# GLA and SSD layers: short products put off by some weight chunks, gate columns two blocks at a time, last output projection with four column blocks at once

## The chip, the cores and the metric

The kernel runs on one core of a Trainium2 chip. The metric is the device time of one execution in microseconds (us). TensorE (PE) multiplies, VectorE (DVE) and ScalarE (ACT) work elementwise, SyncE (SP) issues the weight transfers.

## The reference

Four layers in a row, RWKV, GLA, SSD, RWKV, on 256 tokens of width 2048, all in fp32. Each layer normalizes x, shifts and scales it by a modulation computed from c (`ada_w`), runs its mixer and adds the result to x with a gate. The two mixers that the change touches, cut down:

```python
def gla_mixer(h, ...):             # 4 heads, keys 256, values 512, chunks of 64 tokens
    q, k, v, g, low = split(h @ w_in)
    scores  = (q e^(b - b_ref)) (k e^(b_ref - b))^T            # within a chunk, causal
    o       = scores v + (q e^b) state;  state = state * e^b_last + (k e^(b_last - b))^T v
    return (rms_normalize(o, head_g) * silu(g)) @ w_out

def ssd_mixer(h, ...):             # 64 heads of 64 in 8 groups, state 128, chunks of 128 tokens
    z, xbc, dt = split(h @ w_in)
    xs, bm, cm = split(silu(causal_conv4(xbc)))
    y = (cb * decay)(xs * dt) + (cm prev_state) e^acum + d_skip * xs       # cb = cm bm^T, causal
    y = rms_normalize(y * silu(z), per group of 512)
    return y @ w_out
```

## The kernel before

Every large product is fp32 in three parts: each operand is split into a high and a low half, and hi x hi, lo x hi and hi x lo are summed in one PSUM bank. A weight chunk is 4 k-tiles of 128 rows by 256 columns. SP fetches it (`load_w`, tile `raw`), ACT casts the high half (`split`, L338, tile `H`), DVE subtracts the low half (L340, tile `L`), and PE runs 24 matmuls of 128x256 (`prods`, L393). `H` and `L` have three buffers each, so the cast of a chunk waits until PE has read the chunk three before it. `jobs` takes a list of column blocks of 256 and walks over the k-tiles; `proj` cuts wide projections into blocks and calls `jobs` with one block at a time. A block is accumulated in a bank of `acc`, of which there are two; when its last chunk is issued, its `evac` empties the bank. After each chunk `tick` counts up and, by the table `PACE`, issues the next pieces of the modulation (a transfer from `ada_w` and an `adaacc` product on DVE, L304).

GLA runs head by head: projections of v, q and k, then the short products on five banks of their own (`b1`): scores, values and state (L1167 to L1198, outputs into `O`), a Newton root per token, the transposes of the scaled `O` (L1212), and after that the projection of g, whose `evg` multiplies silu(g) with the turned `O` and splits it into `ys` (L408, L409). SSD runs group by group: bc columns, conv, scores and decay products `M`, xs columns, conv, transposes (L1348), state and values (L1356 to L1370), then z's columns, whose `evz` empties a bank in two halves: ACT takes tanh into `cvt` (L1379), DVE multiplies with the bank (L1380) and with `yv` (L1381). The sum over squares (L1393), a Newton root on DVE (L1041 to L1049), its broadcast (`inv_rms`, L480, L483, L485), the scaling (L1397) and the split into `ys` follow. Heads or groups go in pairs: `paired` hands the eight `ys` tiles of two of them to `outproj`, eight column blocks of two chunks each, before the next part's g or z; the last pair's comes at the layer's end.

The text's order is a priority, not the order on the engines: a list scheduler places each instruction when its inputs and buffers are free by its own estimate, earlier text first. Each engine then runs its list strictly in that order.

Of the kernel before, what the change touches and what calls it, by code (L numbers as in the profile page):

```python
# [9 lines left out]
F32 = mybir.dt.float32  # L10
# [119 lines left out]
class Kern:  # L130
    def __init__(self, ctx, tc, A, out, layers=(0, 1, 2, 3), final=True):
# [15 lines left out]
        self.hold = False  # L147
        self.par = self.const.tile([P, NPAR], F32, name="par")
# [237 lines left out]

    def prods(self, ps, xt, hi, lo, xc, wc, first, last, tokens=False):

        for w, part in ((hi, 0), (hi, 1), (lo, 0)):
            lhs, rhs = w[:, wc], xt[:, part, xc]  # L390
            if tokens:
                lhs, rhs = rhs, lhs
            self.nc.tensor.matmul(ps, lhs, rhs, start=first and part == 0 and w is hi, stop=last and w is lo)  # L393

    def tick(self):

        self.tk += 1
# [18 lines left out]
    def outproj(self, wv, k0, ys, i, norm=None):  # L416
# [10 lines left out]
        for n0 in range(0, D, cols):  # L427
            def evac(j, ps, n0=n0):
# [10 lines left out]
            self.hold = bool(norm) and n0 == D - cols  # L439
            self.proj(wv, n0, cols, ys, evac, k0=k0)  # L440
# [669 lines left out]
    def paired(self, n, part, wout, i):  # L1110

        ys, k0, due = [], 0, []
        for g in range(n):
            ys += part(g, lambda: due and due.pop()())
            if g % 2:
                due.append(lambda ys=ys, k0=k0, norm=self.b1 if g == n - 1 else None:
                           self.outproj(wout, k0, ys, i, norm))
                ys, k0 = [], k0 + 8
        due.pop()()

    def gla_head(self, h, hs, win, bc, due, vt):
# [33 lines left out]
        self.proj(win, 1024 + 256 * h, 256, hs, evk)  # L1155


        HS = (slice(0, 64), slice(64, 128))
        ps = self.b1()
        for s in range(2):  # L1160
            for bi in range(2):
                i = slice((2 * s + bi) * C, (2 * s + bi + 1) * C)
                for kk in range(2):
                    for bj in range(2):
                        j = slice((2 * s + bj) * C, (2 * s + bj + 1) * C)
                        l, r = (ke, qe) if bi == bj else (kn, qs)
                        nc.tensor.matmul(ps[HS[bj], s * P + bi * C:s * P + (bi + 1) * C], l[:, kk, j], r[:, kk, i],  # L1167
                                         start=(kk == 0), stop=(kk == 1))
        sT = gu.tile([P, 2, P], F32, name="sT")
        nc.vector.tensor_scalar(out=sT.rearrange("p c t -> p (c t)"), in0=ps[:, 0:T], scalar1=3e38, scalar2=-3e38,  # L1170
                                op0=ALU.min, op1=ALU.max)
        nc.vector.tensor_tensor(out=sT, in0=sT, in1=self.c("tri128").unsqueeze(1).broadcast_to([P, 2, P]),
                                op=ALU.mult)

        d4 = dec.rearrange("p (k c) o -> p k c o", c=NCH)
        for t, c, o in ((kn, 0, 1), (qs, 3, 2)):
            t = t[:, :, c * C:(c + 1) * C]
            nc.vector.tensor_tensor(out=t, in0=t, in1=d4[:, :, o].broadcast_to([P, 2, C]), op=ALU.mult)

        kt = gu.tile([P, 2, P], F32, name="kt")  # L1180
        ps = self.b1()
        for kk in range(2):
            nc.tensor.transpose(ps[:, kk * P:(kk + 1) * P], kn[:, kk, 0:P], self.c("ident"))
        nc.scalar.copy(out=kt.rearrange("p a c -> p (a c)"), in_=ps[:, 0:T])

        O = gu.tile([P, 2, 512], F32, name="O", bufs=1)
        S = gu.tile([P, 2, 512], F32, name="S")
        for s in range(2):
            ps = self.b1()
            nc.tensor.matmul(ps, sT[:, s, :], vt[:, s, :], start=True, stop=s == 0)  # L1190
            if s:
                for kk in range(2):
                    nc.tensor.matmul(ps, qs[:, kk, P:], S[:, kk, :], start=False, stop=kk == 1)
            nc.scalar.copy(out=O[:, s, :], in_=ps)
            if not s:
                for kk in range(2):
                    ps = self.b1()
                    nc.tensor.matmul(ps, kt[:, kk, :], vt[:, 0, :], start=True, stop=True)  # L1198
                    nc.scalar.copy(out=S[:, kk, :], in_=ps)

        var = gu.tile([P, 2], F32, name="var")
        for tt in range(2):
            sq = gu.tile([P, 512], F32, name="osq", bufs=1)
            nc.scalar.activation(sq, O[:, tt, :], AF.Square)
            nc.vector.tensor_reduce(out=var[:, tt:tt + 1], in_=sq, op=ALU.add, axis=mybir.AxisListType.X)
        rs = self.rsqrt_tiny(var, 1.0 / 512, EPS, gu)
        oT = gu.tile([P, 4, T], F32, name="oT")
        for tt in range(2):
            nc.vector.tensor_scalar(out=O[:, tt, :], in0=O[:, tt, :], scalar1=rs[:, tt:tt + 1], scalar2=None, op0=ALU.mult)
            ps = self.b1()  # L1210
            for v in range(4):
                nc.tensor.transpose(ps[:, v * P:(v + 1) * P], O[:, tt, v * P:(v + 1) * P], self.c("ident"))  # L1212
            for v in range(4):
                nc.scalar.activation(oT[:, v, tt * P:(tt + 1) * P], ps[:, v * P:(v + 1) * P], AF.Copy,
                                     scale=self.p("gla_head_g", v))
# [10 lines left out]
        self.proj(win, 4096 + 512 * h, 512, hs, evg)  # L1226
# [61 lines left out]

    def ssd_group(self, g, hs, win, acd, tk, due):
        nc = self.nc  # L1290
# [4 lines left out]

        def conv_evac(t0, dst, step=1):
            def ev(j, ps):
                cp = su.tile([P, 2, T + 3], F32, name="cvp")
                nc.vector.memset(cp[:, :, 0:3], 0.0)
                nc.scalar.copy(out=cp[:, :, 3:], in_=ps)  # L1300
                for u in range(2):
                    self.conv(t0 + j + u * step, cp[:, u, :], dst[:, j + u, :])
            return ev
        self.proj(win, 8192 + T * g, T, hs, conv_evac(32 + g, bcx, 8))
# [4 lines left out]
                            .rearrange("p (h t) -> p h t", h=8))  # L1309

        ps = self.b1()
        for c in range(2):
            cs = slice(c * C, (c + 1) * C)
            nc.tensor.matmul(ps[:, cs], Bt[:, cs], Ct[:, cs], start=True, stop=True)
        cb = su.tile([P, 2, C], F32, name="cb")
        nc.vector.tensor_tensor(out=cb, in0=ps[:, 0:T].rearrange("p (c t) -> p c t", c=2),
                                in1=self.c("tri128").unsqueeze(1).broadcast_to([P, 2, C]), op=ALU.mult)
        ps = self.b1()
        nc.tensor.transpose(ps[:, 0:C], Bt[:, 0:C], self.c("ident"))
        bk = su.tile([P, C], F32, name="bk")  # L1320
        nc.scalar.copy(out=bk, in_=ps[:, 0:C])

        M = [None, None]
        for c in range(2):
            m = su.tile([P, 8, C], F32, name=f"M{c}", bufs=1)
            for h in range(8):
                nc.vector.tensor_scalar(out=m[:, h, :], in0=ab[:, h, c * C:(c + 1) * C],
                                        scalar1=tk[:, 2 + c, 8 * g + h:8 * g + h + 1], scalar2=0.0,
                                        op0=ALU.subtract, op1=ALU.min)
            nc.scalar.activation(m, m, AF.Exp)  # L1330
            nc.vector.tensor_tensor(out=m, in0=m, in1=cb[:, c, :].unsqueeze(1).broadcast_to([P, 8, C]), op=ALU.mult)
            M[c] = m

        ce = su.tile([P, 8, C], F32, name="ce", bufs=1)
        nc.scalar.activation(ce, ab[:, :, C:], AF.Exp)
        nc.vector.tensor_tensor(out=ce, in0=ce, in1=Ct[:, C:].unsqueeze(1).broadcast_to([P, 8, C]), op=ALU.mult)

        de = su.tile([P, 8], F32, name="de")
        nc.vector.tensor_tensor(out=de, in0=ab[:, :, C - 1], in1=tk[:, 2, HG], op=ALU.subtract)
# [132 lines left out]
```

## Time and profile before

| | |
|---|---|
| median of 3 runs | 2883.41 us (2878.49 to 2889.22) |
| profiled execution | 2887.0 us, span 2885.0 us, mean TensorE clock 0.952 |
| PE busy | 2686.2 us, 93% |
| DVE busy | 2212.4 us, 77% |
| ACT busy | 1392.8 us, 48% |
| GLA | about 905 to 1346 us of the span |
| SSD | about 1346 to 2080 us |

An engine's busy time is what its instructions took; a wait belongs to the instruction at the end of an idle stretch, with the instruction that released it. The clock is a share of full speed: a stretch at 0.50 runs its matmuls half as fast. PE 93% busy includes such stretches.

### The profile page before, as it was taken

How to read it: one execution, taken by the hardware profiler on the slowest of the kernel's cores; microseconds unless marked ns; L12 is line 12 of the kernel's file. 1: busy time of each engine (PE TensorE's matmuls, PEld its weight loads, DVE VectorE, ACT ScalarE, POOL GpSimd, SP SyncE). 2: the span in 40 equal slices, each digit the busy share in tenths (PEclk: the TensorE clock that was granted, in tenths of full speed). 3: DMA queues.
4: the chain of work that ended last, by engine and by line, in shares of the span. 5: the costliest groups of instructions: out<-in, count | busy, mean ns of one | idle time of the engine just before them, and what ended most of it. 6: DMA issues, size and time to landing. Idle time of an engine off the chain costs nothing.

```text
span 2885.0 us, 64064 instructions
## 1 busy us (share of the span) xinstructions
PE 2686.2 (93%) x26098; PEld 2505.1 (87%) x26098; DVE 2212.4 (77%) x3918; ACT 1392.8 (48%) x2315; POOL 154.6 (5%) x298
## 2 busy tenths in 40 slices
PE   6899999999987899988998999999889999999997
PEld 4789889887877899987988999999879988988887
DVE  5778777877788888877898788887668897666666
ACT  3475655433335454434544454554457756453333
POOL 0011110101000000000000000000000111010100
PEclk8899999999998999999999999999989999999999
DMA  9866557977677888976784767776557665585543
GB/s 348 308 231 190 176 161 261 347 266 278 207 261 244 293 285 291 324 268 197 277 294 161 242 219 228 224 226 216 167 171 236 230 208 190 178 297 194 207 132 108
DMA packets 239126, 673.68 MB, mean 234 GB/s; under 512 B 72272, under 2 KB 78416, under 8 KB 235760
## 3 DMA queue, kind: packets, MB, share of 16 engines
q1 hardware_dynamic: 217904, 580.84, 60.2%
q0 software_dynamic: 20928, 88.75, 8.5%
q8 instruction: 205, 3.36, 0.5%
q14 instruction: 89, 0.73, 0.1%
HBM read 620.66 MB, written 48.82 MB: 232 GB/s over the span
## 4 chain that ended last, share of the span: by engine, by line
PE 66%; DVE 8%; DMA 8%; issue 3%; ACT 2%; SPq 1%; POOL 0%; DVEq 0%; ACTq 0%; POOLq 0%
PE acc L393 53%; DMA raw<-in_ada_w 3%; DVE L L340 2%; PE g L785 2%; DVE adaacc L304 1%; ACT H L338 1%; PE b L897 1%; DMA raw<-in_gla_w_in 1%; DMA dx<-bd 1%; DMA raw<-in_rwkv_w_in 1%; PE b L866 1%; DMA raw<-in_rwkv_w_out 1%; PE b L873 1%; DMA sp<-yd 1%; PE b L1030 1%
## 5 line engine op out<-in xcount | busy, mean ns | idle before, releaser
L393 PE MATMUL acc<-xs,H 128*128 128x256 f32 x8480 | 1634.4, 291 | 36.5 <-ACT H L338 8.1
L393 PEld LDWEIGHTS acc<-xs,H 128*128 128x128 f32 x8480 | 1362.8, 196 | 69.3 <-ACT H L338 11.4
L393 PE MATMUL acc<-xs,L 128*128 128x256 f32 x4240 | 1230.6, 291 | 17.1 <-DVE L L340 16.2
L338 ACT CAST H<-raw 128x1024 fp32r<-128x1024 f32 (+1 forms) x706 | 718.0, 1018 | 854.9 <-PE acc L393 634.3
L340 DVE TENSOR_TENSOR L<-raw,H 128x1024 fp32r<-128x1024 f32 (+1 forms) x706 | 833.7, 1183 | 248.9 <-ACT H L338 234.0
L393 PEld LDWEIGHTS acc<-xs,L 128*128 128x128 f32 x4240 | 830.8, 196 | 31.1 <-DVE L L340 21.5
L304 DVE SCALAR_TENSOR_TENSOR adaacc<-raw,cact,adaacc 128x1024 f32<-128x1024 f32 x300 | 384.0, 1280 | 132.6 <-DMA raw<-in_ada_w 130.2
L393 PE MATMUL acc<-ys,H 128*128 128x256 f32 x1536 | 293.3, 291 | 12.2 <-DVE ys L409 4.9
L393 PEld LDWEIGHTS acc<-ys,H 128*128 128x128 f32 x1536 | 245.9, 195 | 22.0 <-issue 6.6
L393 PE MATMUL acc<-ys,L 128*128 128x256 f32 x768 | 222.1, 290 | 0.4 <-DVE L L340 0.4
L393 PEld LDWEIGHTS acc<-ys,L 128*128 128x128 f32 x768 | 149.6, 195 | 4.6 <-issue 3.6
L551 ACT ACTIVATE hn<-x,mod,omu 128x256 f32<-128x256 f32 x192 | 113.4, 599 | 1.5 <-DVE x L542 1.2
L431 DVE SCALAR_TENSOR_TENSOR x<-acc,mod,x 128x256 f32<-128x256 f32 x192 | 83.6, 477 | 35.7 <-PE acc L393 35.3
L393 PE MATMUL acc<-H,xs 128*128 128x256 f32 x512 | 97.1, 290 | 1.6 <-ACT vt L1078 1.6
L554 DVE SCALAR_TENSOR_TENSOR xm<-x,par,hn 128x256 f32<-128x256 f32 x192 | 88.6, 476 | 1.4 <-ACT hn L551 0.3
L393 PEld LDWEIGHTS acc<-H,xs 128*128 128x128 f32 x512 | 82.4, 197 | 3.1 <-ACT vt L1078 1.8
L393 PE MATMUL acc<-L,xs 128*128 128x256 f32 x256 | 73.8, 289 | 0.0
L785 PE MATMUL g<-abkp 64*128 64x128 f32 x768 | 65.8, 293 | 4.0 <-DVE G L823 2.7
L408 ACT CAST xs<-xm 128x256 fp32r<-128x256 f32 x128 | 50.9, 400 | 35.4 <-DVE xm L554 33.0
L785 PEld LDWEIGHTS g<-abkp 64*128 64x128 f32 x768 | 52.2, 190 | 15.8 <-issue 8.8
L1284 DVE SCALAR_TENSOR_TENSOR cva<-cvp,hcw,cva 128x256 f32<-128x256 f32 x144 | 64.9, 476 | 0.0
L278 DVE SCALAR_TENSOR_TENSOR adaacc<-raw,cact,adaacc 128x512 f32<-128x512 f32 x56 | 41.9, 748 | 27.5 <-DMA raw<-in_ada_w 23.0
(358 smaller groups left out, 3063.0 us busy)
## 6 DMA issues: line engine op xcount, KB each, us to landing
raw<-in_ada_w SPq DMA_DIRECT2D x384, 512.0 KB, 4.8
raw<-in_rwkv_w_in SPq DMA_DIRECT2D x256, 512.0 KB, 4.7
raw<-in_ssd_w_in SPq DMA_DIRECT2D x128, 512.0 KB, 4.4
raw<-in_gla_w_in SPq DMA_DIRECT2D x96, 512.0 KB, 5.2
raw<-in_ssd_w_out SPq DMA_DIRECT2D x64, 512.0 KB, 4.2
raw<-in_rwkv_w_out SPq DMA_DIRECT2D x48, 512.0 KB, 4.2
abkp<-kd POOLq DMA_DIRECT2D x16, 1024.0 KB, 7.3
raw<-in_gla_w_out SPq DMA_DIRECT2D x32, 512.0 KB, 4.9
```

Source lines behind the costliest of these rows:

```text
L278: nc.vector.scalar_tensor_tensor(out=acc, in0=raw[:, u, :], scalar=self.cact[:, k:k + 1], in1=acc, op0=ALU.mult, op1=ALU.add)
L304: nc.vector.scalar_tensor_tensor(out=acc, in0=raw, scalar=self.cact[:, k:k + 1], in1=acc, op0=ALU.mult, op1=ALU.add)
L338: nc.scalar.copy(out=hi, in_=raw[:, a:a + n])
L340: nc.vector.tensor_tensor(out=lo, in0=raw[:, a:a + n], in1=hi, op=ALU.subtract)
L393: self.nc.tensor.matmul(ps, lhs, rhs, start=first and part == 0 and w is hi, stop=last and w is lo)
L408: nc.scalar.copy(out=t[:, 0, :], in_=src)
L431: nc.vector.scalar_tensor_tensor(out=self.x[:, t, 1:], in0=ps[:, u, :], scalar=gate[:, t:t + 1], in1=self.x[:, t, 1:], op0=ALU.mult, op1=A ...
L551: nc.scalar.activation(t1, x[:, k, 1:], AF.Identity, scale=self.omu[:, col:col + 1], bias=self.mods[(i, 0)][:, k:k + 1])
L554: done[k] = nc.vector.scalar_tensor_tensor(out=xm, in0=x[:, k, 0:T], scalar=self.p("rwkv_mu", col), in1=t1, op0=ALU.mult, op1=ALU.add)
L785: self.nc.tensor.matmul(ps[h][:, n * C:(n + 1) * C], s[r, q, c * C:(c + 1) * C], t[r, q, c * C:(c + 1) * C], start=True, stop=True)
L866: nc.tensor.matmul(ps[r, n * H:(n + 1) * H], G[h][:, q, r], tk[:, 2, q, HS[h]], start=not c, stop=not c or h == 1)
L1284: nc.vector.scalar_tensor_tensor(out=a, in0=src[:, k:k + T], scalar=w[k], in1=a, op0=ALU.mult, op1=ALU.add)
```

## The change

- `tick` gets a list of parts that are put off: `put_off(n, part)` holds a part until n more chunks have been issued, `run_later()` runs all that are left.
- GLA: scores 1 tick after q and k, values and state 3, transposes of `O` 6.
- SSD: scores and `M` 3 ticks after bc; transposes of xs 3 ticks after xs, state 5, values 6; the sum over squares 3 ticks after z and the scaling 5, for which `inv_rms` is cut in two.
- g of GLA and z of SSD: one `jobs` call with both column blocks, chunk by chunk in turn, so that both `acc` banks fill together.
- Last `outproj` of GLA and of SSD: the first four column blocks in one call, two of them in two of the five `b1` banks (`pairs`), so that the last part's own `ys` are first needed after four chunks; what is put off is run when they are asked for.
- bc's transpose shares the bank of the SSD scores.

```diff
+    def put_off(self, n, part):
+        self.later.append((self.tk + n, part))
+    def run_later(self, tk=math.inf):
+        while self.later and self.later[0][0] <= tk:
+            self.later.pop(0)[1]()
...
-            self.proj(wv, n0, cols, ys, evac, k0=k0)
+        blocks = [(n0, cols, taker(n0), cols, False) for n0 in range(0, D, cols)]
+        if lead:
+            n = len(lead) + 2
+            self.jobs(wv, blocks[:n], ys, k0, banks=lead)
+            blocks = blocks[n:]
+        for block in blocks:
+            self.hold = bool(norm) and block is blocks[-1]
+            self.jobs(wv, [block], ys, k0)
...
+        def out(g, ys):
+            def rows(k):
+                if k >= len(ys[k // 4]) + k // 4 * 4:
+                    self.run_later()
+                return ys[k // 4][k % 4]
+            last = g == n - 1
+            self.outproj(wout, 4 * g - 4, Lazy(8, rows), i, self.b1 if last else None,
+                         self.pairs(self.b1, 2) if last else ())
...
+        self.put_off(1, scores)
+        self.put_off(3, lambda: box.append(values()))
+        self.put_off(6, lambda: turned(box[0]))
...
-        self.proj(win, 4096 + 512 * h, 512, hs, evg)
+        self.jobs(win, [(4096 + 512 * h + T * n, T, lambda _, ps, n=n: evg(2 * n, ps), T, False) for n in range(2)], hs)
...
+        self.put_off(3, scores)
...
+        self.put_off(3, turned)
+        self.put_off(5, states)
+        self.put_off(6, values)
...
-        self.proj(win, 512 * g, 512, hs, evz)
+        self.jobs(win, [(512 * g + T * n, T, lambda _, ps, n=n: evz(2 * n, ps), T, False) for n in range(2)], hs)
...
+        self.put_off(3, sums)
+        self.put_off(5, scaled)
```

How the lists of the engines change, at three places. First ACT at the end of z of SSD group 2, before (`H` is the cast of a weight chunk, `cvt` the read of half a z bank):

```order
948 L338 CAST H<-raw 128x1024 x13
949 L1379 ACTIVATE cvt<-acc 128x256
950 L338 CAST H<-raw 128x1024
951 L1379 ACTIVATE cvt<-acc 128x256
952 L1384 ACTIVATE ss<-yv 128x256
953 L338 CAST H<-raw 128x1024
954 L1387 ACTIVATE cva<-yv 128x256
955 L338 CAST H<-raw 128x1024 x2
```

and of the change:

```order
954 L339 CAST H<-raw 128x1024 x14
955 L1431 ACTIVATE cvt<-acc 128x256
956 L339 CAST H<-raw 128x1024
957 L1431 ACTIVATE cvt<-acc 128x256
958 L1436 ACTIVATE ss<-yv 128x256
959 L1431 ACTIVATE cvt<-acc 128x256
960 L1439 ACTIVATE cva<-yv 128x256
961 L1431 ACTIVATE cvt<-acc 128x256
```

The four reads of the group now stand together; between the first bank's two reads there is a cast as before, but z's two banks now close one chunk apart, before four.

DVE at the same place, before:

```order
1765 L340 TENSOR_TENSOR L<-raw,H 128x1024
1766 L1380 SCALAR_TENSOR_TENSOR cvt<-cvt,acc 128x256
1767 L1381 SCALAR_TENSOR_TENSOR yv<-cvt,yv 128x256
1768 L340 TENSOR_TENSOR L<-raw,H 128x1024
1769 L1380 SCALAR_TENSOR_TENSOR cvt<-cvt,acc 128x256
1770 L1381 SCALAR_TENSOR_TENSOR yv<-cvt,yv 128x256
```

and of the change:

```order
1768 L341 TENSOR_TENSOR L<-raw,H 128x1024 x4
1769 L1432 SCALAR_TENSOR_TENSOR cvt<-cvt,acc 128x256
1770 L305 SCALAR_TENSOR_TENSOR adaacc<-raw,cact,adaacc 128x1024
1771 L1433 SCALAR_TENSOR_TENSOR yv<-cvt,yv 128x256
1772 L341 TENSOR_TENSOR L<-raw,H 128x1024
1773 L1432 SCALAR_TENSOR_TENSOR cvt<-cvt,acc 128x256 x2
```

The first bank's second multiply (first of row 1773) stands behind one more L and, here, an adaacc.

PE at SSD's end, before (`ys` rows are output projection, `b` a `b1` bank, L1393 the sum over squares, L483 the broadcast of the root):

```order
9150 L393 MATMUL acc<-ys,L 128x256
9151 L393 MATMUL acc<-ys,H 128x256 x2
9152 L393 MATMUL acc<-ys,L 128x256
9153 L1393 MATMUL b_24519<-cst,ss 128x1 x2
9154 L483 MATMUL b_24540<-xm,cst 128x256
9155 L393 MATMUL acc<-ys,H 128x256 x3
```

and of the change:

```order
9166 L398 MATMUL acc<-ys,H 128x256 x2
9167 L398 MATMUL acc<-ys,L 128x256
9168 L1447 MATMUL b_24611<-cst,ss 128x1 x2
9169 L512 MATMUL b_24672<-xm,cst 128x256
9170 L398 MATMUL b_24511<-ys,H 128x256
9171 L398 MATMUL b_24512<-ys,H 128x256
```

The sum and the broadcast still stand next to each other, ahead of the group's own `ys`. Between z and the sum there are now four chunks of 24 matmuls, before two.

## Rows read from the trace of the kernel before

**Rows 1.** The page, busy times and shares of the span.

```profile
PE 2686.2 (93%) x26098; PEld 2505.1 (87%) x26098; DVE 2212.4 (77%) x3918; ACT 1392.8 (48%) x2315; POOL 154.6 (5%) x298
```

**Rows 2.** Stretches: from:to, length, busy (x count) by engine, clock, DMA, GB/s.

```profile
1284.00:1346.00 62.00, 57.13 (x404) 49.98 (x404) 40.71 (x54) 24.51 (x43) 0.00 (x0) 0.89 0.65 210
1430.00:1600.00 170.00, 154.04 (x1269) 147.48 (x1268) 144.90 (x278) 81.33 (x122) 1.59 (x3) 0.94 0.68 232
1600.00:1700.00 100.00, 100.00 (x836) 98.10 (x837) 77.59 (x121) 47.86 (x67) 0.00 (x0) 1.00 0.70 228
2040.00:2080.00 40.00, 31.21 (x236) 28.70 (x235) 25.56 (x52) 15.06 (x25) 0.00 (x0) 0.83 0.45 150
```

**Rows 3.** Waits of PE, 1276 to 1300: total us, times, longest.

```profile
PE b L1212 <- DVE O L1209: 3.3, 1, 3.3
PE acc L393 <- ACT ys L408: 2.6, 2, 2.3
PE acc L393 <- DVE ys L409: 1.6, 1, 1.6
PE acc L393 <- DVE gth L1222: 0.5, 1, 0.5
```

**Rows 4.** Stretches of the clock, columns as in rows 2.

```profile
1285.10:1298.70 13.60, 8.84 (x36) 7.86 (x36) 8.66 (x14) 4.20 (x14) 0.00 (x0) 0.50 0.57 187
2063.30:2066.70 3.40, 3.40 (x18) 3.40 (x17) 1.97 (x3) 0.42 (x1) 0.00 (x0) 0.50 0.67 224
2070.10:2080.40 10.30, 6.31 (x24) 5.33 (x25) 4.84 (x19) 1.97 (x5) 0.00 (x0) 0.50 0.17 52
295.20:298.60 3.40, 3.40 (x19) 3.40 (x18) 3.30 (x13) 3.34 (x10) 0.15 (x1) 0.50 0.10 11
1006.00:1012.00 6.00, 6.00 (x54) 6.00 (x53) 5.34 (x9) 3.49 (x11) 0.00 (x0) 1.00 0.87 313
```

**Rows 5.** Timeline at SSD's end: start, length, engine, line, instruction, idle before and releaser.

```profile
2060.30 1.04 ACT L338 CAST H<-raw 128x1024 fp32r<-128x1024 f32 x1 [1.55 <-issue]
2061.25 0.38 ACT L1379 ACTIVATE cvt<-acc 128x256 f32<-128x256 f32 x1
2061.38 1.23 DVE L340 TENSOR_TENSOR L<-raw,H 128x1024 fp32r<-128x1024 f32 x1 [0.85 <-ACT H L338]
2062.52 0.41 DVE L1380 SCALAR_TENSOR_TENSOR cvt<-cvt,acc 128x256 f32<-128x256 f32 x1
...
2062.99 0.55 PE L393 MATMUL acc<-ys,H 128*128 128x256 f32 x2 [2.65 <-DVE cvt L1380]
...
2072.38 1.19 PE L483 MATMUL b<-xm,cst 128*128 128x256 f32 x2 [4.43 <-DVE xm L480]
...
2074.99 0.80 PE L393 MATMUL acc<-ys,H 128*128 128x256 f32 x2 [1.42 <-ACT ys L408]
```

**Rows 6.** Waits of PE, 1600 to 2040.

```profile
PE acc L393 <- DVE L L340: 0.4, 1, 0.4
```

**Rows 7.** The page, costliest groups: busy us, mean ns, idle before.

```profile
L304 DVE SCALAR_TENSOR_TENSOR adaacc<-raw,cact,adaacc 128x1024 f32<-128x1024 f32 x300 | 384.0, 1280 | 132.6 <-DMA raw<-in_ada_w 130.2
```

**Rows 8.** Timeline of PE at 293 and at 1005.

```profile
293.38 0.69 PE L1011 MATMUL b<-Tn,LT 32*32 32x32 f32 x16 [2.03 <-DVE Tn L995]
...
1005.38 0.50 PE L393 MATMUL acc<-H,xs 128*128 128x256 f32 x2 [1.62 <-ACT vt L1078]
```

**Rows 9.** Timeline of PE and DVE, SSD groups 0 and 1.

```profile
1437.84 0.50 PE L393 MATMUL acc<-xs,H 128*128 128x256 f32 x2 [1.26 <-DVE cvt L1380]
...
1512.19 0.50 PE L393 MATMUL acc<-xs,H 128*128 128x256 f32 x2 [2.84 <-DVE cvt L1380]
1513.25 2.35 DVE L1331 TENSOR_TENSOR M<-M,cb 128x1024 f32<-128x1024 f32 x2
1515.52 1.42 DVE L409 TENSOR_TENSOR ys<-yv,ys 128x256 fp32r<-128x256 f32 x4
...
1531.17 0.51 PE L393 MATMUL acc<-xs,H 128*128 128x256 f32 x2 [1.55 <-ACT cvp L1300]
```

More of the change, by code (lines that the diff above doesn't have):

```diff
@@ L385, in jobs, with pairs @@
                     evac(0, bank[:, 0:nj])
+    def pairs(self, bank, n):
+        return [bank().rearrange("p (j t) -> p j t", j=2) for _ in range(n)]
     def prods(self, ps, xt, hi, lo, xc, wc, first, last, tokens=False):
@@ L414, in parts, with outproj @@
         return t
-    def outproj(self, wv, k0, ys, i, norm=None):
+    def outproj(self, wv, k0, ys, i, norm=None, lead=()):
         nc = self.nc
@@ L425, in outproj, with taker, evac @@
         cols = 2 * P
-        for n0 in range(0, D, cols):
-            def evac(j, ps, n0=n0):
+        def taker(n0):
+            def evac(j, ps):
                 for u in range(ps.shape[1]):
@@ L1155, in gla_head @@
         self.proj(win, 1024 + 256 * h, 256, hs, evk)
[L1158 to L1168, printed above, removed]
@@ L1180, in gla_head @@
[L1180 to L1184, printed above, removed]
+        sT = gu.tile([P, 2, P], F32, name="sT")
         O = gu.tile([P, 2, 512], F32, name="O", bufs=1)
-        S = gu.tile([P, 2, 512], F32, name="S")
-        for s in range(2):
+        oT = gu.tile([P, 4, T], F32, name="oT")
@@ L1189, in gla_head, with scores @@
+        def scores():
+            HS = (slice(0, 64), slice(64, 128))
             ps = self.b1()
[L1190 to L1209, printed above, removed]
-            ps = self.b1()
[L1211 to L1215, printed above, removed]
+            for s in range(2):
+                for bi in range(2):
+                    i = slice((2 * s + bi) * C, (2 * s + bi + 1) * C)
+                    for kk in range(2):
+                        for bj in range(2):
+                            j = slice((2 * s + bj) * C, (2 * s + bj + 1) * C)
+                            l, r = (ke, qe) if bi == bj else (kn, qs)
+                            nc.tensor.matmul(ps[HS[bj], s * P + bi * C:s * P + (bi + 1) * C], l[:, kk, j], r[:, kk, i],
+                                             start=(kk == 0), stop=(kk == 1))
@@ L1287, in conv, with conv_evac, ev @@
         nc.vector.scalar_tensor_tensor(out=dst, in0=th, scalar=1.0, in1=a, op0=ALU.add, op1=ALU.mult)
+    def conv_evac(self, t0, dst, step=1):
+        nc = self.nc
+        def ev(j, ps):
+            cp = self.su.tile([P, 2, T + 3], F32, name="cvp")
+            nc.vector.memset(cp[:, :, 0:3], 0.0)
+            nc.scalar.copy(out=cp[:, :, 3:], in_=ps)
+            for u in range(2):
+                self.conv(t0 + j + u * step, cp[:, u, :], dst[:, j + u, :])
+        return ev
     def ssd_group(self, g, hs, win, acd, tk, due):
@@ L1294, in ssd_group @@
         bcx = su.tile([P, 2, T], F32, name="bc")
[L1296 to L1304, printed above, removed]
+        self.proj(win, 8192 + T * g, T, hs, self.conv_evac(32 + g, bcx, 8))
         Bt, Ct = bcx[:, 0, :], bcx[:, 1, :]
@@ L1319, in ssd_group @@
-        nc.tensor.transpose(ps[:, 0:C], Bt[:, 0:C], self.c("ident"))
         bk = su.tile([P, C], F32, name="bk")
[L1321 to L1332, printed above, removed]
+        M = [su.tile([P, 8, C], F32, name=f"M{c}", bufs=1) for c in range(2)]
@@ L1346, in ssd_group, with states, values @@
+        yv = su.tile([P, 4, T], F32, name="yv")
+        def states():
             ps = self.b1()
+            nc.tensor.matmul(ps, bk, xd.rearrange("p h d -> p (h d)"), start=True, stop=True)
+            nc.scalar.copy(out=xd.rearrange("p h d -> p (h d)"), in_=ps)
+        def values():
             for v in range(4):
-                nc.tensor.transpose(ps[:, v * P:(v + 1) * P], xT[:, v, c * C:(c + 1) * C], self.c("ident"))
-            t = su.tile([P, 8, 64], F32, name=f"xc{c}")
-            nc.vector.tensor_tensor(out=t, in0=ps.rearrange("p (h d) -> p h d", d=64),
-                                    in1=tk[:, c, HG].unsqueeze(2).broadcast_to([P, 8, 64]), op=ALU.mult)
@@ new lines, in values @@
+                hr = [(2 * v + u, slice(64 * u, 64 * u + 64)) for u in range(2)]
+                for h, r in hr:
+                    nc.tensor.matmul(ps[r, 0:C], xc[0][:, h, :], M[0][:, h, :], start=True, stop=True)
+                for h, r in hr:
+                    nc.tensor.matmul(ps[r, C:T], xc[1][:, h, :], M[1][:, h, :], start=True, stop=False)
+                for h, r in hr:
+                    nc.tensor.matmul(ps[r, C:T], xd[:, h, :], ce[:, h, :], start=False, stop=True)
+                nc.vector.scalar_tensor_tensor(out=yv[:, v, :], in0=xT[:, v, :], scalar=self.p("ssd_d", 4 * g + v),
+                                               in1=ps[:, 0:T], op0=ALU.mult, op1=ALU.add)
```

155 lines of the change are left out of this document (99 added, 56 removed).

## The prediction

> **What bounds the kernel now.** I read the busy times of the page first: PE works 93% of the span, DVE 77%, ACT 48% [rows 1]. So only PE's idle time and its clock can be saved, and the table by stretches says where they are. From 1600 to 1700 us, in SSD, PE is busy for all of the stretch at clock 1.00 (836 matmuls in 100 us: 0.120 us each, 2.9 us for a weight chunk of 24); nothing is to be won there, and any new wait is a loss in full. Time is lost at 1284-1346 (end of GLA), 1430-1600 (SSD groups 0 and 1) and 2040-2080 (end of SSD) [rows 2].
>
> The waits give the sizes. At GLA's end PE waits 3.3 + 2.6 + 1.6 + 0.5 = 8.0 us [rows 3], and the clock then stands at 0.50 for 13.6 us [rows 4], of which half, 6.8, is lost. At SSD's end it waits 2.65, 4.43 and 1.42 [rows 5], 8.5 in all, with 3.4 + 10.3 us at 0.50 [rows 4]: 6.9 lost. In the busy middle of SSD, from 1600 to 2040 us, one wait of 0.4 us is all [rows 6].
>
> The row that decides my forecast is the wait of 2.65 us that ends at 2062.99 [rows 5]. There z's second block of columns is followed by only one chunk into the other bank, 24 matmuls, before the next block wants the bank back. The bank is emptied in two halves, and by the order on the two engines the second half comes after a weight cast: ACT casts H at 2060.30 and reads the bank at 2061.25, DVE subtracts L at 2061.38 and only then, at 2062.52, does the second multiply; PE starts at 2062.99. A cover of 24 matmuls does not suffice where the usual 96, 11.5 us, do.
>
> **The change part by part.** PE's matmuls, the weight chunks and the pace of the modulation stay, so its 384 us of adaacc on DVE [rows 7] stay too. What changes is order.
>
> *g of GLA and z of SSD, two blocks chunk by chunk.* Both banks now close within one chunk of each other, and the next job wants the first one 24 matmuls after it closed. This is the situation at 2062.99, now at the ends of GLA heads 0, 1, 2 and of SSD groups 2 to 6, eight times, and in the changed order ACT's second read stands behind one more cast, which waits for the buffer of the last chunk, and DVE's second multiply behind that L. Price of one: from the cast's start at 2060.30 to PE's at 2062.99 it is 2.69 us [rows 5]; the buffer comes free two matmuls, 0.24, before the chunk's end, which leaves 2.45. The wait measured 2.65, and I take that: 8 x 2.65 = 21.2 (bounds 19.6 and, with an adaacc of 1.28 [rows 7] in the way at two places, 23.8). The waiting matmul holds all of PE behind it; the casts after it need buffers that PE gives back, so nothing runs ahead meanwhile.
>
> *The clock after these waits.* After the wait of 2.65 us the granted clock fell to 0.50, the lower level of 1.2 GHz, for 3.4 us; the same followed a wait of 2.03 us at 293; after 1.62 us at 1005 it stayed at 1.00 [rows 4, 5, 8]. So one new wait costs 0 or 1.7 us more. By the nearer rows most fall; I take six of eight: 10.2 (bounds 0 and 13.6). The Trainium skill, "TensorE: Matmul & The Clock Gate", section "A second HAM failure mode: psum-queue depth-cycling", says that a kernel which cycles through banks and leaves PE idle briefly between groups swings between the two levels and pays at each swing; the rows at 293 and 2062.99 agree, the one at 1005 does not, and by the rule this term would be 13.6.
>
> *SSD group 0.* z's bank already costs 1.26 us at 1437.84 [rows 9]; in the new order a cast, an L (1.23) and an adaacc (1.28) stand ahead of the second multiply: 1.04 + 1.23 + 1.28 + 0.41 is about 4 us from the last chunk's end [rows 5, 7], +2.7, and a clock fall of 1.7. Bounds 0 and +4.4.
>
> *SSD group 1.* Before, PE waits 2.84 us for the second multiply, until 1512.19, and the M products come after it [rows 9]. The new order puts both M products (2.35), four ys differences (1.42), two xc products and two Ls (2 x 1.23) ahead of it, 6.2 us without xc; PE would resume about 8 us after it is ready, +5, and the wait of 1.55 that ends at 1531.17 goes: +3.4. Bounds 0 and +6. The waits at about 1410, 1457 and 1566 keep their places and causes in the order: 0, plus or minus 2.
>
> *GLA's end.* Turning O is put off by six ticks and the four-block lead gives 96 matmuls of cover instead of 24. But the order keeps the transposes behind only 24 ys matmuls, and the new bank wait stands ahead of these: 2.65 us in place of 3.3. The rest of the chain is then covered by 48 more matmuls; I leave 0.5 + 0.7 for H and L cast late and 1.8 for the second g bank, late behind an adaacc. Idle 8.0 becomes 5.6: -2.4. The long stretch at half clock should split into short ones, 5 us in all: -4.3. Together -6.7 (bounds 0, if the waits only change places, and -14.8, 8.0 + 6.8, if all goes).
>
> *SSD's end.* 96 matmuls now stand between z and the group's own ys, the first 48 in banks of their own, so the wait of 2.65 and its 3.4 us at half clock go: -4.3. But the sum over the squares stands behind all 96 in PE's queue, with the broadcast of the inverse root as the next instruction: the chain sums, Newton steps, broadcast, yv, ys still runs while PE has nothing else. The 4.43 and 1.42 stay, with their 10.3 us at 0.50. Bounds 0 and -15.4 (8.5 + 6.9: all gone).
>
> *Put-off scores, values, states elsewhere.* They land in stretches that are 100% busy on PE: 0. The last RWKV layer's order shifts a little: 0, plus or minus 5.
>
> **Sum.** +21.2 + 10.2 + 4.4 + 3.4 - 6.7 - 4.3 = +28.2 us. The profiled execution took 2887.0 us (span 2885.0), 3.6 above the median: 2887.0 + 28.2 - 3.6 = 2911.6. Forecast 2911.
>
> **Rivals.** *A, faster.* The lead covers both ends and the bank waits stay away, because z's first half is emptied while the second block's last chunk runs. For it: in the middle of SSD DVE was rarely late [rows 6]. Against it: the 2.65 us that the same order of the queues cost [rows 5], and the cast can't be earlier, since its buffer is in use. The page "Perfetto Trace Analysis" of the Trainium skill, "Matmul Optimizations", speaks for A: it wants all banks in use, and the lead takes four where two were; its section "Matmuls" speaks against it, since groups are to rotate through banks so that emptying one overlaps the next group, and two banks that close together don't. The time: both ends by their far bounds, -30, with groups 0 and 1 at 0: 2853; with the ends at my values, -11: 2872. Chance 0.13.
> *B, no change that counts.* The bank waits come at 2.45 us, the clock stays up after all but one (+1.7), groups 0 and 1 cost 3 together, and the ends give 18: 19.6 + 1.7 + 3 - 18 = +6: 2890. For it: the wait of 1.62 us without a fall [rows 8]. Decided by whether the Newton chain at SSD's end gets cover. Chance 0.22.
> *C, worse.* Every wait pulls the clock, groups 0 and 1 at their upper bounds, the ends only change places: 23.8 + 13.6 + 10.4 - 4.3 = +43.5: 2927. Chance 0.15.
> *My forecast*, bank waits of about 2.6 us with most of them followed by half clock: 0.50.
>
> **How the numbers follow.** What a measurement of this kernel can tell from no change is about 0.5%, 14.4 us: the bounds are 2869 and 2898. Of A about two in ten lies between 2869 and 2872: faster 0.11. B is within, and of the forecast's own spread (2896 to 2922) a small part: same 0.25. The rest of the forecast and C: slower 0.64. The range leaves out A and the far end of C: 2880 to 2928.
>
> **What would show it.** In the profile after: PE's waits in SSD groups 2 to 6 on "DVE cvt", five of 2.3 to 2.8 us, where there was one of 0.4 on anything; three on "DVE gth" in GLA; short dips of the granted clock behind most. At SSD's end no wait on cvt, but one of 4 to 5 us on xm. At GLA's end a wait on gth of 2 to 3 us in front of the first ys, and little or none at the transposes of O. PE's busy time at full clock unchanged. I am wrong if PE stays 100% busy from 1600 us to SSD's end, or if the wait on xm is gone.

## The result, and the profile after

The changed kernel takes 2929.4 us (median of 4 runs, 2926.8 to 2934.7) against 2886.3 for the kernel before beside it; the ratio is 1.0156, 95% interval 1.0129 to 1.0182. It is slower by about 43 us. The forecast was 2911 with a range to 2928: the direction and the place were right, the size fell short, and the time lies just outside the range.

The profiled execution of the changed kernel took 2934.7 us (span 2932.8), 47.7 longer than the one before. Cut at the broadcasts of the layers' norms, and at the end of the span, the lengths in us are:

| | RWKV, first | GLA | SSD | RWKV, last | rest |
|---|---|---|---|---|---|
| before | 887.1 | 469.0 | 775.9 | 740.7 | 12.2 |
| after | 886.7 | 477.9 | 803.4 | 751.7 | 13.0 |
| difference | -0.4 | +8.9 | +27.5 | +11.0 | +0.8 |

The page's busy times say little of it: PE's is 13 us longer in a span that is 48 us longer, and the other engines work as they did [rows 1]. The clock alone does not explain it: the time at 0.50 is 84 us before and 100 after in GLA and SSD, and 279 against 275 in the whole program.

```profile
PE 2698.9 (92%) x26098; PEld 2507.7 (86%) x26098; DVE 2215.9 (76%) x3918; ACT 1390.8 (47%) x2315; POOL 154.0 (5%) x298
```

The waits do. PE's waits in the changed kernel from 900 to 1320 us (GLA's heads and end; `gth` is what g's bank is read into, as `cvt` for z's); columns: us in total, times, longest:

```profile
PE acc L398 <- DVE gth L1267: 8.3, 4, 2.6
```

and from 1320 to 2140 us (SSD):

```profile
PE acc L398 <- DVE cvt L1432: 29.7, 7, 7.5
PE b L512 <- DVE xm L505: 10.5, 2, 6.3
PE b L1398 <- DVE xT L1332: 4.7, 2, 3.3
PE b L398 <- ACT ys L422: 2.8, 1, 2.8
```

From 1600 to 2100 us, the busy middle of SSD, where one wait of 0.4 us stood [rows 6], there are now:

```profile
PE acc L398 <- DVE cvt L1432: 17.2, 5, 4.6
PE acc L398 <- DVE L L341: 1.0, 1, 1.0
```

And the stretch that was 100% busy [rows 2] has 64 matmuls fewer in it (stretch, length, busy and count of PE, PEld, DVE, ACT, POOL, clock, DMA, GB/s):

```profile
1600.00:1700.00 100.00, 95.79 (x772) 94.25 (x772) 71.14 (x123) 45.34 (x62) 0.53 (x1) 0.97 0.65 211
```

The timeline at the end of z of SSD group 3 shows what one such wait is (start, length, engine, line, instruction, idle before and releaser):

```profile
1722.20 1.04 ACT L339 CAST H<-raw 128x1024 fp32r<-128x1024 f32 x1
...
1723.14 0.37 ACT L1431 ACTIVATE cvt<-acc 128x256 f32<-128x256 f32 x1
...
1724.36 1.04 ACT L339 CAST H<-raw 128x1024 fp32r<-128x1024 f32 x1
1724.41 0.41 DVE L1432 SCALAR_TENSOR_TENSOR cvt<-cvt,acc 128x256 f32<-128x256 f32 x1
1724.86 0.43 DVE L1433 SCALAR_TENSOR_TENSOR yv<-cvt,yv 128x256 f32<-128x256 f32 x1
1725.31 0.38 ACT L1431 ACTIVATE cvt<-acc 128x256 f32<-128x256 f32 x1
1725.43 1.23 DVE L341 TENSOR_TENSOR L<-raw,H 128x1024 fp32r<-128x1024 f32 x1
...
1726.58 0.75 DVE L1432 SCALAR_TENSOR_TENSOR cvt<-cvt,acc 128x256 f32<-128x256 f32 x2
1727.04 0.50 PE L398 MATMUL acc<-xs,H 128*128 128x256 f32 x2 [2.65 <-DVE cvt L1432]
```

It is the wait of [rows 5] again, to the hundredth of a microsecond: the bank's first half is read at 1723.14, the second at 1725.31 behind a cast, and multiplied at 1726.58 behind that cast's L. At the end of group 6 the same order holds one thing more:

```profile
2023.86 1.28 DVE L305 SCALAR_TENSOR_TENSOR adaacc<-raw,cact,adaacc 128x1024 f32<-128x1024 f32 x1 [1.83 <-DMA raw<-in_ada_w]
2025.07 0.41 DVE L1433 SCALAR_TENSOR_TENSOR yv<-cvt,yv 128x256 f32<-128x256 f32 x1
2025.40 1.22 DVE L341 TENSOR_TENSOR L<-raw,H 128x1024 fp32r<-128x1024 f32 x1
...
2026.54 0.74 DVE L1432 SCALAR_TENSOR_TENSOR cvt<-cvt,acc 128x256 f32<-128x256 f32 x2
2027.00 0.80 PE L398 MATMUL acc<-xs,H 128*128 128x256 f32 x2 [4.64 <-DVE cvt L1432]
```

A step of the modulation stands on DVE in front of all that is left of the emptying, and it waits 1.83 us for its own weights to arrive. DVE takes its instructions in order, so the bank, and PE, wait for a transfer that has nothing to do with them.

### The profile page after: what moved, and what is told of

It is laid out like the page before. It is cut to its first block, busy times and chain, and to the rows that moved or that the text cites. A ratio compares the mean times of both kernels' runs of the same rounds, so it can differ in the third digit from the quotient of the medians.

```text
span 2932.8 us, 64075 instructions
## 1 busy us (share of the span) xinstructions
PE 2698.9 (92%) x26098; PEld 2507.7 (86%) x26098; DVE 2215.9 (76%) x3918; ACT 1390.8 (47%) x2315; POOL 154.0 (5%) x298
## 4 chain that ended last, share of the span: by engine, by line
PE 59%; DVE 11%; DMA 11%; issue 4%; ACT 2%; SPq 1%; POOL 0%; DVEq 0%; ACTq 0%; POOLq 0%
PE acc L398 46%; DMA raw<-in_ada_w 6%; DVE L L341 4%; DVE adaacc L305 2%; PE g L814 2%; ACT H L339 1%; DMA dx<-bd 1%; PE b L398 1%; DMA raw<-in_rwkv_w_out 1%; PE b L926 1%; DMA raw<-in_gla_w_in 1%; PE b L895 1%; PE b L902 1%; SPq L1001 0%; DVE xs L423 0%
## 5 line engine op out<-in xcount | busy, mean ns | idle before, releaser
L398 PE MATMUL acc<-ys,H 128*128 128x256 f32 x1408 | 268.6, 290 | 6.8 <-DVE gth L1267 5.2
L398 PEld LDWEIGHTS acc<-ys,H 128*128 128x128 f32 x1408 | 224.3, 194 | 17.0 <-issue 9.0
L398 PE MATMUL acc<-ys,L 128*128 128x256 f32 x704 | 203.2, 289 | 0.0
L398 PEld LDWEIGHTS acc<-ys,L 128*128 128x128 f32 x704 | 136.1, 193 | 3.5 <-issue 3.3
L814 PEld LDWEIGHTS g<-abkp 64*128 64x128 f32 x768 | 52.2, 190 | 17.2 <-issue 9.4
```

Source lines behind the costliest of these rows:

```text
L814: self.nc.tensor.matmul(ps[h][:, n * C:(n + 1) * C], s[r, q, c * C:(c + 1) * C], t[r, q, c * C:(c + 1) * C], start=True, stop=True)
```

## The experiments

Each time is a median; the ratio is to the kernel before, run beside it on the same chip, with its 95% interval. Layer lengths are from the profiles, one execution each.

**One block after the other.** Everything else of the change stays, with shorter put-offs, which this order needs.

```diff
-        self.put_off(6, lambda: turned(box[0]))
+        self.put_off(4, lambda: turned(box[0]))
-        self.jobs(win, [(4096 + 512 * h + T * n, T, lambda _, ps, n=n: evg(2 * n, ps), T, False) for n in range(2)], hs)
+        self.proj(win, 4096 + 512 * h, 512, hs, evg)
-        self.put_off(5, states)
-        self.put_off(6, values)
+        self.put_off(4, states)
+        self.put_off(4, values)
-        self.jobs(win, [(512 * g + T * n, T, lambda _, ps, n=n: evz(2 * n, ps), T, False) for n in range(2)], hs)
+        self.proj(win, 512 * g, 512, hs, evz)
```

> The change, but g of GLA and z of SSD one column block after the other as before; so that their inputs are there in time, the transposes of O are put off by 4 ticks instead of 6, SSD states and values by 4 instead of 5 and 6. Theory of the prediction (the two banks that close together cost the time): no wait on cvt or gth of over 1 us in SSD groups 2 to 6 and GLA heads 0 to 2; the time falls by 25 to 40 us, to 2890 to 2905, or lower if the ends gain. Rival (put-off products crowd DVE, or the lead costs): stays at 2920 or more. If the last RWKV layer's 11 us more in the profile come from its changed order and not from chance, they may stay here: 2895 to 2905.

Measured: 2887.4, ratio 1.0019 [1.0001, 1.0036]; GLA 466.9, SSD 777.8 us. No wait for `cvt` stands between 1600 and 2060 us. Without the pairs the loss is gone, but for 0.2%.

**The pairs alone, in the kernel before.**

```diff
-        self.proj(win, 512 * g, 512, hs, evz)
+        self.jobs(win, [(512 * g + T * n, T, lambda _, ps, n=n: evz(2 * n, ps), T, False) for n in range(2)], hs)
```

and the same for g.

> The kernel before with nothing of the change but g and z two column blocks chunk by chunk. Theory: waits on cvt of 2.6 to 4.8 us at SSD groups 2 to 6 as in the changed kernel, and the time rises by 25 to 45 us, to 2910 to 2930. Rival (put-offs and lead cost the time): within 8 us of before, 2880 to 2894.

Measured: 2918.9, ratio 1.0123 [1.0099, 1.0148]; GLA 479.6, SSD 804.0 us, as in the changed kernel. The waits for `cvt` are 27.7 us in eight. The pairs alone make most of the loss.

**The pair in two other banks.** The two blocks go to two of the five `b1` banks, so the next job does not want their banks.

```diff
-        ..., T, False) for n in range(2)], hs)
+        ..., T, False) for n in range(2)], hs, banks=self.pairs(self.b1, 2))
```

> The change, but the pair of g or z blocks is summed in two of the five b1 banks and not in the acc banks, so that the next job finds its bank free; order of the chunks and put-offs stay. Theory: the waits on cvt and gth at the next job's first matmul go, and with them the half clock behind them; time 2885 to 2900 unless short products now wait for the three banks that are left (waits on b). Rival (the chunk order itself or the put-offs cost): 2920 or more.

Measured: 2880.6, ratio 0.9997 [0.9982, 1.0012]; GLA 462.9, SSD 774.0 us. That is below the 2885 to 2900 expected. No wait for `cvt` or `gth` is left. In sum the order chunk by chunk costs nothing; what costs is that the next block wants the bank back 24 matmuls later. One new wait stood in SSD, on the modulation's sum:

```profile
1479.69 1.08 PE L311 MATMUL mx<-adaacc,cst 128*32 128x256 f32 x8 [9.48 <-DVE adaacc L305]
```

**Without the lead of four blocks.**

```diff
-                         self.pairs(self.b1, 2) if last else ())
+                         ())
```

> The change without the four-block lead in the last output projection of GLA and SSD (one column block at a time). Prediction's terms: at SSD's end the wait on cvt of about 2.7 us comes back with 3.4 us of half clock, at GLA's end the chain of ys; 5 to 11 us slower than the changed kernel, 2934 to 2941. Rival, the lead gives nothing (its chain still stands behind it in PE's list): within 4 us of 2929.

Measured: 2922.1, ratio 1.0136 [1.0107, 1.0166], beside 1.0156 [1.0129, 1.0182] for the whole change. Both expectations missed: without the lead the kernel is not slower but, if anything, faster, though the intervals overlap. The wait for `cvt` at SSD's end is back, 2.61 us at 2096.76; SSD takes 806.5 against 803.4 us, GLA 477.6 against 477.9. What the lead brings is at most some 3 us at SSD's end and nothing at GLA's. The last RWKV layer takes 738.6 us in this profile against 751.7, more than the lead's share; more on that layer at the end of the account below.

**z's bank emptied in one round.** One tanh and one multiply over both halves; GLA is left as it was.

```diff
+            both = su.tile([P, 2, T + 3], F32, name="cvp")[:, :, 0:T]
+            nc.scalar.activation(both, ps, AF.Tanh, scale=0.5)
+            nc.vector.scalar_tensor_tensor(out=both, in0=both, scalar=1.0, in1=ps, op0=ALU.add, op1=ALU.mult)
             for u in range(2):
                 v = j + u
-                th = su.tile([P, T], F32, name="cvt")
-                nc.scalar.activation(th, ps[:, u, :], AF.Tanh, scale=0.5)
-                nc.vector.scalar_tensor_tensor(out=th, in0=th, scalar=1.0, in1=ps[:, u, :], op0=ALU.add, op1=ALU.mult)
+                th = both[:, u, :]
```

> The changed kernel, with z's bank in the SSD groups emptied by one tanh and one multiply over both halves (512 columns each) in place of two of each over 256; GLA as it was. Theory (the bank is late because its emptying is two rounds on ACT and DVE, and a weight's cast or subtraction, or a modulation step, comes between the rounds): at most one of these is left ahead of each of the two instructions, so by the rows 1.04 + 0.6 + 1.23 + 0.75 = 3.6 us after the last product against 2.9 us of products in the other bank. The six waits for cvt (29.7 us in the changed kernel's profile) fall to under 1 us each, most falls of the clock behind them go, the SSD layer comes from 803 to about 780 us and the time from 2929 to 2900-2912. Rival (two banks that close 2.9 us apart are too few however they are emptied): the waits stay at 2 us and more, and the time at 2922-2932.

Measured: 2893.3, ratio 1.0032 [1.0015, 1.0049]; SSD 772.7 us, shorter than before the change, GLA 479.0 as in the changed kernel. The theory holds, and the time lies below the range that it gave; of the bank waits two are left, one of 1.7 us where under 1 was expected. The waits of PE from 1600 to 2060 us:

```profile
PE acc L398 <- DVE L L341: 2.3, 3, 1.2
PE acc L398 <- DVE cvp L1430: 2.1, 2, 1.7
```

and the end of z of group 2:

```profile
1639.42 1.05 ACT L339 CAST H<-raw 128x1024 fp32r<-128x1024 f32 x1 [1.83 <-PE acc L398]
...
1640.37 0.59 ACT L1429 ACTIVATE cvp<-acc 128x512 f32<-128x512 f32 x1
...
1640.50 1.23 DVE L341 TENSOR_TENSOR L<-raw,H 128x1024 fp32r<-128x1024 f32 x1 [1.66 <-ACT H L339]
...
1641.64 0.68 DVE L1430 SCALAR_TENSOR_TENSOR cvp<-cvp,acc 128x512 f32<-128x512 f32 x1
...
1642.47 0.47 PE L398 MATMUL acc<-xs,H 128*128 128x256 f32 x2
```

One cast, one tanh, one L, one multiply: from 1639.42 to 1642.32 that is 2.90 us, the length of the 24 matmuls that cover it, and PE goes on. The same cover that was 2.65 us short with two rounds suffices here with one. The Trainium skill, "Perfetto Trace Analysis", section "Optimizing Scalar/DVE Operations", says that grouping into larger operations can pay where the engine is saturated; here neither engine is (DVE 76% busy, ACT 47% in the changed kernel), and the two instructions were shortened by little (0.59 for twice 0.38, 0.68 for twice 0.41). What went is the cast and the L that the order puts between two rounds, 2.3 us.

**The modulation halted during z's pair.**

```diff
+        self.hold = True
         self.jobs(win, [(512 * g + T * n, T, lambda _, ps, n=n: evz(2 * n, ps), T, False) for n in range(2)], hs)
+        self.hold = False
```

> The changed kernel, with the modulation's steps halted during the eight chunks of each SSD group's z pair, and made up behind them at no more than two a chunk. Theory (waits above 2.65 us are a modulation step on DVE that itself waits for its transfer, or a step that stands in the row ahead of the emptying): groups 2 and 6 fall from 4.2 and 4.6 to 2.3-2.9, groups 0 and 1 (5.1 and 7.5) fall too, and the others stay at 2.6-3.1; the sum of the waits comes from 29.7 to about 16-20, the time from 2929 to 2914-2922. Rival (the steps made up later are late elsewhere, at the group's BC convolution or the transposes): the sum of all PE waits in the layer stays, and so does the time, 2925-2932.

Measured: 2917.6, ratio 1.0118 [1.0085, 1.0152]. The time lies where the theory put it, but the interval overlaps that of the changed kernel, and in the profile, which is of the longest of the four executions, SSD takes 804.8 us, no less than there. The sum of the waits for `cvt` fell as expected, to 18.9 us, and groups 0 and 1 have none; but the two waits of groups 2 and 6 grew: the first step after the halt is issued right at the end of z, where its weights are still on their way.

```profile
1648.53 1.28 DVE L305 SCALAR_TENSOR_TENSOR adaacc<-raw,cact,adaacc 128x1024 f32<-128x1024 f32 x1 [2.74 <-DMA raw<-in_ada_w]
...
1651.67 0.58 PE L398 MATMUL acc<-xs,H 128*128 128x256 f32 x1 [5.56 <-DVE cvt L1432]
...
2025.44 1.28 DVE L305 SCALAR_TENSOR_TENSOR adaacc<-raw,cact,adaacc 128x1024 f32<-128x1024 f32 x1 [3.56 <-DMA raw<-in_ada_w]
...
2028.58 0.80 PE L398 MATMUL acc<-xs,H 128*128 128x256 f32 x2 [6.66 <-DVE cvt L1432]
```

So the run is not shown to be a cure, but it is a dose of the suspected cause. In the changed kernel, group 2:

```profile
1652.77 1.28 DVE L305 SCALAR_TENSOR_TENSOR adaacc<-raw,cact,adaacc 128x1024 f32<-128x1024 f32 x1 [1.38 <-DMA raw<-in_ada_w]
...
1655.91 0.80 PE L398 MATMUL acc<-xs,H 128*128 128x256 f32 x2 [4.20 <-DVE cvt L1432]
```

Four pairs are at hand, the step's wait for its transfer and PE's wait for the bank: 1.38 and 4.20, 1.83 and 4.64 in the changed kernel, 2.74 and 5.56, 3.56 and 6.66 here. PE's wait is 2.8 to 3.1 us longer than the transfer's in each. The runs with the pairs alone, without the lead and with short put-offs give six more, with transfer waits of 1.11 to 1.95 us, and PE's is 2.8 us longer in all of them. A fifth place of this run, group 4, has the step ahead of the bank's first multiply, not the second: 1.38 and 3.74, 2.4 longer. In the changed kernel a wait without a step in between is 2.6 to 3.1 us, so the step's wait counts in full and of its 1.28 us of work little shows. The rival, that the waits come back elsewhere, is right for SSD in this profile.

**Shorter put-offs, the rest as changed** (4 in place of 6 in GLA, 4 and 4 in place of 5 and 6 in SSD).

> The changed kernel with shorter put-offs, turned after 4 chunks in place of 6 in GLA, states and values after 4 in place of 5 and 6 in SSD: the control to the single-block run, which needed these. Theory (put-offs are worth nothing either way, the pairs are all): 2925-2932, waits for cvt and gth as in the changed kernel, about 38 us together. Rival (the long put-offs, which bring the group's results close to z's evacuation, are part of the loss): under 2918.

Measured: 2929.9, ratio 1.0158 [1.0122, 1.0194]; waits for `cvt` 28.8 us in seven, for `gth` 8.0 in four. No effect of the put-offs' length is seen, so the single-block run is to be read as the pairs alone.

**Other banks, and the halt.** The pair in two `b1` banks, with the halt above.

> The kernel with the pair in two banks of b1, plus the modulation halted during each SSD group's z pair. In the run without the halt one new wait stood in the SSD layer: PE reached the modulation's sum (mx) 9.5 us before DVE had finished it, with 13.7 us at half clock. Theory (that wait is the modulation falling due among group 0's work on DVE, and goes when it is moved): 2864-2872, faster than both kernels. Rival (DVE is behind there whatever the order, and PE meets the wait at the next instruction that needs DVE): 2876-2884.

Measured: 2881.2, ratio 0.9996 [0.9977, 1.0014]. The rival holds. The wait on the modulation's sum went and came back as a wait of 8.5 us on `xm`, the operand of the broadcast of a group's root, here group 0's; SSD takes 785.7 us in this profile, longer than without the halt. The one-round run has such a wait at group 1's root, 8.64 us at 1567.82. This fits that DVE is behind by that much in groups 0 and 1, 85% busy from 1430 to 1600 us [rows 2], and that PE pays for it at whichever instruction needs DVE next.

**Both cures.** GLA's pair in two `b1` banks, z's bank in SSD in one round.

> The changed kernel with both of the cures that worked alone: GLA's pair in two banks of b1 (GLA took 462.9 us with it), and z's bank in SSD emptied over both halves at once (SSD took 772.7 us with it). Theory (each layer keeps its own result): 2883 - 6 - 3 = about 2874, 2868-2880, faster than both kernels by a little. Rival (the layers' differences of 3 to 6 us are within what single profiles of the same instructions differ by): 2880-2886, the same as the kernel before.

Measured: 2874.5, ratio 0.9977 [0.9959, 0.9995]; GLA 462.5, SSD 772.5 us. It is faster than both kernels, than before by 0.2%, which is less than half of what was called a measurable difference ahead of the result; 12 runs of it and 23 of before make the interval, which just leaves out 1.

**One round alone, in the kernel before.**

> The kernel before with one edit alone: z's bank in the SSD groups emptied over both halves at once. Theory (before, a bank has 96 products, over 10 us, until it is wanted again, so how it is emptied costs nothing): 2878-2886, the same, SSD at 774-778 us. Rival (the shorter emptying is a gain by itself on the two groups whose cvt waits stood there, 6.8 us in three, and at the SSD end): 2868-2876.

Measured: 2880.5, ratio 0.9995 [0.9975, 1.0015]. The same time, as the theory said. In its profile SSD is shorter (764.6 us), for which the rival spoke, and the last RWKV layer longer (750.4); the medians show no gain, though the interval has room for 0.25%. Behind the pairs the same edit brought the ratio from 1.0156 to 1.0032. So one round is worth that much only where the next block wants the bank 24 matmuls later.

## Why the prediction was right in direction and short in size

What a stretch costs is counted here by how late a kernel starts its n-th matmul, in profile time, against the n-th of the kernel before; all have 26098. The places are times of the kernel before.

*The bank waits (+21.2): the mechanism was right, the sum partly by luck.* In SSD they stand where they were put, and the experiments show the cause from three sides: other banks remove them, one round all but removes them, the pairs alone make them. SSD groups 2 to 6 wait 17.2 us where 13.25 was the sum for five, because in groups 2 and 6 the adaacc in the way waits for its transfer. The order had shown that adaacc between the two multiplies, and the bound took only its 1.28 us of work: the wait ahead of it was left out. GLA heads 0 to 2 wait 2.57, 0 and 0.44 us where 7.95 was the sum for three. In heads 1 and 2 PE starts the next block 2.7 us after the last product of g as well (at 1077.85 and 1208.26), but its list has the modulation's sum in between, and in head 1 the transposes of `O`. That a waiting PE has nothing else to do, as the prediction had it, depends on what the list holds at that place. In all it is 20.2 us, near 21.2 because the excess in SSD and the lack in GLA cancel.

*The clock after them (+10.2): the same sum, by luck.* Six falls of 3.4 us were forecast behind eight waits. There are four: 6.8 + 3.4 + 6.8 us at 0.50 from 1600 to 2100 us and 3.4 behind GLA's head 0, together the 20.4 us of six short ones. After the waits of 4.20, 3.06 and 4.64 us the granted clock fell to 0.50, the level of 1.2 GHz; after 2.65 and 2.61 it stayed at 1.00:

```profile
1654.30:1661.10 6.80, 5.19 (x24) 5.19 (x25) 4.41 (x11) 2.10 (x6) 0.00 (x0) 0.50 0.48 160
1727.00:1733.00 6.00, 5.96 (x49) 5.96 (x50) 4.21 (x10) 2.34 (x6) 0.00 (x0) 1.00 0.59 204
1840.00:1846.00 6.00, 6.00 (x50) 6.00 (x51) 5.13 (x10) 2.52 (x6) 0.00 (x0) 1.00 0.38 105
```

But the same 2.65 us had a fall behind it at 2062.99 [rows 4, 5], and 2.57 us at 994.80, GLA's head 0, and the 2.61 and 2.64 at GLA's end have one too. The length of a wait alone does not decide it, and what else does was not tried. The rule weighed in the prediction, from the Trainium skill, "TensorE: Matmul & The Clock Gate", section "A second HAM failure mode: psum-queue depth-cycling", by which each swing is paid for, agrees with the trace where the clock fell and has nothing on the waits where it did not.

Half of a stretch at 0.50 is also too much for what it loses. Three products start in 0.64 us there, in 0.36 at 1.00:

```profile
1657.36 0.63 PE L398 MATMUL acc<-xs,H 128*128 128x256 f32 x2
1657.78 0.41 PE L398 MATMUL acc<-xs,L 128*128 128x256 f32 x1
1658.00 0.63 PE L398 MATMUL acc<-xs,H 128*128 128x256 f32 x2
...
1661.53 0.40 PE L398 MATMUL acc<-xs,H 128*128 128x256 f32 x2
1661.77 0.28 PE L398 MATMUL acc<-xs,L 128*128 128x256 f32 x1
1661.89 0.40 PE L398 MATMUL acc<-xs,H 128*128 128x256 f32 x2
```

So a product takes 0.213 us in place of 0.120, not twice as long, and 44% of the time that PE works in such a stretch is lost; its idle time in there stands among the waits already. At GLA's end before, PE worked for 8.84 of the 13.6 us [rows 4], which loses 3.9 us and not 6.8.

*SSD groups 0 and 1 (+4.4 and +3.4): the waits are larger, the sum smaller.* The two waits are 5.1 and 7.5 us, each with 6.8 us at 0.50. But waits before were said to keep their places and partly did not: 3.4 us at 1457 became 1.6, 3.0 at 1570 became 0.8, and of the 17.0 us at half clock there 6.8 are left. The changed kernel is 8.6 us late ahead of the two groups (1358.8) and 11.2 behind them (1600): they cost 2.6 us more, not 7.8. The four runs without these bank waits (the pair in other banks with and without the halt, one round, both cures) each have one wait of 8.4 to 9.5 us in these groups.

*GLA's end (-6.7) is the step that failed in kind, and not only in size.* The transposes' wait of 3.3 us [rows 3] went, and the bank wait stands before the first `ys`, as said. But the second g bank costs not 1.8 but a full wait too. Its emptying stands on ACT behind the turned `O`, two casts and the first bank's `ys`, so its first read comes at 1303.15, and PE waits for its last multiply:

```profile
1303.15 0.38 ACT L1266 ACTIVATE gth<-acc 128x256 f32<-128x256 f32 x1
...
1308.06 0.80 PE L398 MATMUL acc<-ys,H 128*128 128x256 f32 x2 [2.64 <-DVE gth L1267]
```

The clock falls at both waits:

```profile
1289.10:1295.90 6.80, 6.11 (x28) 6.11 (x29) 4.62 (x11) 0.80 (x1) 0.00 (x0) 0.50 0.95 346
1306.20:1313.00 6.80, 4.95 (x23) 4.95 (x24) 4.27 (x7) 0.81 (x2) 0.00 (x0) 0.50 0.55 196
```

That is 13.6 us in two pieces where it was one of 13.6 [rows 4]; the 5 us "in all" that the step took for it had no row behind it. PE's idle time did fall, from 8.0 to 6.4 us, most of the 2.4 that were forecast. The 4.3 of the clock failed: PE works for 11.1 us in the two pieces, which loses 4.8 where 3.9 were lost before. The changed kernel is 9.2 us late before GLA's end (1276) and 9.3 behind it (1345): the end gave nothing. With the bank waits removed it gives a part: in the three runs with GLA's pair in other banks the end gains 2.1 to 3.7 us by this count, and GLA takes 462.5 to 462.9 us, 6 less than before, the rest of it in the heads. With one block after the other, where the lead and shorter put-offs stay, the end gains 0.1 us.

*SSD's end (-4.3): the path came as forecast, the gain smaller.* No `cvt` wait stands there, and the broadcast waits on:

```profile
2111.95 1.19 PE L512 MATMUL b<-xm,cst 128*128 128x256 f32 x2 [4.18 <-DVE xm L505]
...
2115.91 0.80 PE L398 MATMUL b<-ys,H 128*128 128x256 f32 x2 [2.78 <-ACT ys L422]
...
2111.70:2121.90 10.20, 7.10 (x28) 6.12 (x29) 4.31 (x10) 1.96 (x5) 0.00 (x0) 0.50 0.26 91
```

By the count (from 38.3 us late at 2050 to 36.0 at 2131) it gains 2.3 us; the wait for the split `ys` is 2.78 where it was 1.42, since yv stands behind an adaacc that waits 1.95 us for its transfer.

*The rest (0).* GLA's heads lose 9.5 us where bank waits and clock make some 4.7; the remainder is a handful of waits of 1 to 1.6 us for H, for L and for the modulation's sum, which the prediction had at nothing. The last RWKV layer, "0, plus or minus 5", is 11.0 us longer in this profile. Its order is another one in nearly every kernel here. The run with short put-offs has the same lists of ACT and DVE in it as the changed kernel, and takes 750.4 us against 751.7, with like waits. The longest is

```profile
2467.82 0.58 PE L398 MATMUL acc<-xs,L 128*128 128x256 f32 x1 [5.96 <-DVE L L341]
```

in the changed kernel, and with short put-offs:

```profile
2460.43 0.58 PE L398 MATMUL acc<-xs,L 128*128 128x256 f32 x1 [6.21 <-DVE L L341]
```

The runs with other banks and the halt and with both cures, again alike in this layer, take 738.3 and 738.5 us; the other orders lie between 738.6 and 750.4. This speaks for the shifted order as the cause, and then the term was mis-sized by some 10 us. It is not shown: no run changes this order alone, and the first layer, alike in all kernels, varies as much.

So of the 19.5 us that the profiles differ beyond the forecast's 28.2, 6.8 are GLA's end, 7.5 groups 2 to 6 (27.2 by the count against 13.25 + 6.4), 2.0 SSD's end and 11 the last layer; the heads and groups 0 and 1 cost 2.2 and 5.2 less than was allowed for, and 0.4 goes the other way in the rest. The medians differ by 43.1, so 4.6 of it is this one execution's. Rival C, 2927, was nearest to the time, but not by its own account: it had every wait pull the clock, where four of eight did; groups 0 and 1 at 10.4, where they cost 2.6; and nothing in the last layer. Only GLA's end changed places as it said. That its number is near is luck.

## What to carry to other kernels

When accumulations are interleaved so that all their banks close together, count what the next user of the first bank still has as cover (here 24 matmuls, 2.9 us) and lay the emptying's instructions against it in the order of each engine, with what stands between them: the work in between cost more than the emptying itself. Before adding banks, try to empty a bank in one round, so that nothing can be queued between two halves. An instruction that stands between two steps of an emptying counts with its own wait for data, not with its length only: here that wait counted in full.

## What was not expected of the hardware

One multiply over 512 columns on DVE took 0.68 us and one tanh on ACT 0.59, against 0.41 and 0.38 over 256: the half costs well over half. Single layers of this program differ by 10 us and more between executions in which their instructions are the same: the first RWKV layer ended between 874.6 and 888.1 us in the profiles of the kernels here, none of which changes it.
